# Three borders of a hybrid attention and feed-forward layer, with the work in another order: gated outputs in stages, one norm for all tokens, early fetches of sums

## The chip, the cores and the metric

One core of a Trainium2 chip runs the whole layer. The metric is the device time of one execution in microseconds; a version's time is the median of three runs. The kernel's own engines are TensorE (PE in the profile, with its weight loads as PEld), VectorE (DVE), ScalarE (ACT), GpSimd (POOL) and SyncE (SP). SP, ACT and POOL also issue the transfers between HBM and the on-chip memory.

## What is computed

The input is 256 tokens of 2048 numbers, all in fp32. `ya` is the mixed output of three groups of dilated attention with 8 heads, `o` that of a gated linear attention with 4 heads, `gr`, `m_a` and `m_b` are slices of the input's first projection.

```python
yb = (o.reshape(b, s, G_DV) * jax.nn.silu(gr)) @ w_proj_b
ya = ya.reshape(b, s, A_WIDTH) @ w_proj_a
y = jax.nn.sigmoid(m_a) * ya + jax.nn.sigmoid(m_b) * yb
x = _layernorm(ALPHA * x + y @ w_out, ln1_g, ln1_b)
ffn = (jax.nn.silu(conv(x @ w_gate)) * (x @ w_up)) @ w_down
x = _layernorm(ALPHA * x + ffn, ln2_g, ln2_b)
```

## The kernel before

**Products.** Every fp32 operand of a product is split into a rounded high part and the low rest: `split` (L138) makes the high part on ACT (L139) and the rest on DVE (L140). A product is three matmuls: high by high, high by low, low by high (L266, L267, L268 in chunks of 512 columns; L230 and L232, or L250 and L253, in tiles of 128 columns). Weights come in pieces of 512 KB, loaded by SP into a ring: `home` (L142) names the ring, either `raw` with 4 buffers or `quarter` with 12 (L851 and L1135 switch it). A piece is split into `whi` (6 buffers) and `wlo` (4 buffers). In a chunk, a piece feeds 12 matmuls: `a_chunk` (L279) runs over the pieces of 512 output columns for both halves of the tokens (t = 0, 1; 128 tokens each).

**Order.** Each engine runs its instructions in a fixed order. The order comes from a scheduler that places the instructions of the program by its own costs and dependencies; the program gives it hints. One hint is the list `side`: `pump` (L188) takes one or more entries from it after every step of a chunk (4 blocks of 128 rows), so that small work lies between the products; `drain` (L196) empties it. On-chip tiles come from rings: `blk` holds 512 numbers in each partition, `tmp` 256, `res` the large operands (8 buffers). Three pools follow each other, early, late and last, and the first user of a new pool waits for the users of the pool before it (L852, L976).

**The first border** lies behind the projections. Two chunks `m` (L845) compute the last quarter pair of `m_b`; beside them runs the rest of the last attention head. The list `side` then holds `gated_stage` (L831): fetch `gr` and `o` of one head of the gated attention (L820), multiply sigmoid(gr) by gr by o (L823), transpose the result into `OB` (L786). After that come the product with w_proj_b (chunks `pb`, L880 to L886; the operands are OB) and the product with w_proj_a (chunks `yp`, L888 on; the operands are `YA2`, which `ya_parts`, L867, fetches and splits beside the pb chunks). Their sums go into `YT`, the operands of w_out.

**The second border** is the first norm. The chunks `wo` of w_out run for n = 0, 1, 2 with both halves of the tokens; for n = 3 (L960 on) the first half of the tokens is finished first, and `normalised(0)` (L930) lies beside the products of the second half. `normalised` takes mean and scale, normalises (L935, ACT), transposes (L939, PE), applies gain and bias (L942, DVE), splits into X1 (L944 ACT, L945 DVE) and spills an fp32 copy X1F to HBM (POOL). Four matmuls on `keep` (L973) lie between.

**The third border** is the feed-forward part's start. Two groups of four pairs of tiles (`fg`, `fu`) run as plain products. Beside the second and later tiles, `sums` (L1125) prepares the operands of the seven-product scheme that the later groups use: for each of 4 quarters one entry fetches four pieces of X1F (ACT issues the transfers, L1131) and the next entry forms sums (L309 to L312, DVE) and splits them (`comb`). Later, `down_group` (L1057) accumulates the product with w_down over six parts; the sums of a part are spilled and fetched again; those of the fifth part come back into the tiles `acc` (L1160).

Of the kernel before, what the change touches and what calls it, by code (L numbers as in the profile page):

```python
# [17 lines left out]
P = 128  # L18
S = 256
D = 2048  # L20
NH = 8
# [39 lines left out]
def hybrid_layer(ctx: ExitStack, tc: tile.TileContext, wp, xt, wgl, gw, par, relb, onehot, rows, xk, out):  # L61
# [134 lines left out]
    def drain():  # L196
        while side or slow:
            pump()
# [586 lines left out]

    def transposed(name, n, halves_of_tokens, gain=None):  # L786
# [33 lines left out]
    def gated_get(h):  # L820
        got[h] = [(fetch("gr", GR[h][t]), fetch("o", O[h][t])) for t in range(2)]

    def gated_mul(h):  # L823
        for t, (x, o) in enumerate(got[h]):
            sg = blk("sg")
            nc.scalar.activation(sg, x, AF.Sigmoid)
            nc.vector.tensor_tensor(x, x, o, op=ALU.mult)
            nc.vector.tensor_tensor(sg, sg, x, op=ALU.mult)
            got[h][t] = sg

    def gated_stage(i):  # L831

        def f():
            if i < GH:
                gated_get(i)
            if 0 <= i - 1 < GH:
                gated_mul(i - 1)
            if 0 <= i - 2 < GH:
                OB.extend(transposed("ob", i - 2, got[i - 2], P_NG))
        return f  # L840


    side.extend(gated_stage(i) for i in range(GH + 2))
    for n in range(2):
        pss = a_chunk("m", xop, 16, AT["mb"] + 8 * n, 2)  # L845
        for t in range(2):
            c = blk("mc")
            nc.scalar.activation(c, pss[t], AF.Copy)
            M[1][2 + n][t] = spill("ms", c)
    drain()  # L850
    home[:] = "quarter", 12  # L851
    early.close()  # L852
    late = ExitStack()
    now[:] = late.enter_context(tc.tile_pool(name="late", bufs=1)), (17, 10, 1)
# [3 lines left out]
    def gate(br, n, t):  # L858
        g = fetch("m", M[br][n][t])
        last_gate[:] = [nc.scalar.activation(g, g, AF.Sigmoid)]  # L860
        return g


    YA2 = [res("ya") for _ in range(2)]
    yaf = {}

    def ya_parts(h):  # L867
        def f():
            if h < NH:
                yaf[h] = fetch("yaf", YA[h], tmp)  # L870
            if h:
                y = YA2[(h - 1) // 4][:, (h - 1) % 4]
                split(y[:, :S], y[:, S:], yaf[h - 1])
        return f

    side.extend(ya_parts(h) for h in range(NH + 1))
    yop = lambda kc: YA2[kc // 4][:, kc % 4]


    yb = []  # L880
    for n in range(4):
        g = [gate(1, n, t) for t in range(2)]
        pss = a_chunk("pb", by_pairs(OB), 16, AT["pb"] + 8 * n)
        for t in range(2):
            nc.vector.tensor_tensor(g[t], g[t], pss[t], op=ALU.mult)
        yb.append(g)  # L886
    drain()
    YT = []  # L888
    for n in range(4):
        g = [gate(0, n, t) for t in range(2)]  # L890
        pss = a_chunk("yp", yop, 8, AT["pa"] + 4 * n)
        for t in range(2):
            y = g[t]
            nc.vector.tensor_tensor(y, y, pss[t], op=ALU.mult)
            nc.vector.tensor_tensor(y, y, yb[n][t], op=ALU.add)
        side.append(lambda n=n, y=g: YT.extend(transposed("yt", n, y)))
# [25 lines left out]
    def residual(n, t, ps):  # L922
        r = R[t][n]
        nc.vector.scalar_tensor_tensor(r, r, ALPHA, ps, op0=ALU.mult, op1=ALU.add)
        nc.vector.bn_stats(stats[t][:, n, :], r)

    X1 = [res("x1") for _ in range(4)]
    X1F = [[None] * 4 for _ in range(2)]

    def normalised(t):  # L930

        _, rs, ms = mean_and_scale(t)
        for n in range(4):
            r = R[t][n]
            nc.scalar.activation(r, r, AF.Identity, scale=rs, bias=ms)  # L935
            pt = bank("pt")
            x1 = blk("x1f").rearrange("p (k t) -> p k t", k=4)
            for k in range(4):
                nc.tensor.transpose(pt[:, k * P : (k + 1) * P], r[:, k * P : (k + 1) * P], ident)  # L939
            for k in range(4):  # L940
                d = 4 * n + k
                nc.vector.tensor_scalar(x1[:, k], pt[:, k * P : (k + 1) * P], pc(P_L1G + d), pc(P_L1B + d), op0=ALU.mult, op1=ALU.add)  # L942
            hi, lo = X1[n][:, :, t * P : (t + 1) * P], X1[n][:, :, S + t * P : S + (t + 1) * P]
            main = nc.scalar.activation(hi, x1, AF.Copy)  # L944
            nc.vector.tensor_tensor(lo, x1, hi.bitcast(F32), op=ALU.subtract)  # L945
            X1F[t][n] = spill("x1s", x1)
            if n == 2:
                held = main
        return held

    yt = by_pairs(YT)
    for n in range(4):
        for t in range(2):
            R[t].append(blk("r"))
            nc.gpsimd.dma_start(R[t][n], xk[t * P : (t + 1) * P, n * 512 : (n + 1) * 512])
        if n < 3:
            pss = a_chunk("wo", yt, 16, AT["wo"] + 8 * n)
            for t in range(2):
                residual(n, t, pss[t])
# [361 lines left out]
```

## Time and profile before

| | |
|---|---|
| median of 3 runs | 1906.82 us (1903.97 to 1907.84) |
| the profiled execution | 1901.4 us, its span 1899.4 us |
| PE busy | 1826.8 us (96%), its clock 0.988 of full in the mean |
| DVE busy | 1449.1 us (76%) |
| ACT busy | 1089.3 us (57%) |
| DMA | 480.64 MB, 253 GB/s in the mean |

72.6 us of the span are without a matmul. In the PE's row of the 40 slices of the span, nearly all of them show 9 tenths; which stretches are not filled is read from the idle time before each group of matmuls and from windows of a few microseconds.

### The profile page before, as it was taken

Reading aid. Unit: us, or ns where it says so; the run is one execution under the profiler, and the core shown is the slowest. Engines: PE = TensorE matmul, PEld = TensorE weight load, DVE = VectorE, ACT = ScalarE, POOL = GpSimd, SP = SyncE. Lnnn points to the kernel's source line nnn. Section 1 sums busy time; section 2 is a strip of 40 time slices with the busy share of each in tenths; the row PEclk is TensorE's granted clock in tenths of the full one; section 3 lists DMA queues with packets and bytes.
Section 4 is the critical chain, followed back from the end, with each engine's and each line's share of the span. In section 5 each row is a group of like instructions: output and inputs, shape, how many; then the busy total and the mean of one; then the engine's idle time right before and its main releaser. Section 6 shows DMA issues by size and latency. Waiting matters only on the chain.

```text
span 1899.4 us, 25463 instructions
## 1 busy us (share of the span) xinstructions
PE 1826.8 (96%) x8974; PEld 1525.4 (80%) x8974; DVE 1449.1 (76%) x1731; ACT 1089.3 (57%) x1400; POOL 236.5 (12%) x349
## 2 busy tenths in 40 slices
PE   8999998999999999998999999899999999999996
PEld 6877887888888888886888878788888888888784
DVE  6968997788797978964656666786597787877977
ACT  6655765565666657654644445565565556555552
POOL 0112111111111311101300000001011110110211
PEclk9999999999999999999999999999999999999998
DMA  8898987978889897897766437569679769778683
GB/s 302 277 304 231 302 283 215 324 213 294 279 249 334 216 316 255 255 333 240 285 220 219 166 112 276 190 172 323 225 203 340 241 199 343 222 232 331 200 283 120
DMA packets 148492, 480.64 MB, mean 253 GB/s; under 512 B 17905, under 2 KB 30220, under 8 KB 148364
## 3 DMA queue, kind: packets, MB, share of 16 engines
q1 hardware_dynamic: 96764, 345.09, 50.9%
q0 software_dynamic: 33456, 115.48, 24.8%
q10 hardware_dynamic: 18144, 18.46, 3.1%
q8 instruction: 70, 1.15, 0.2%
q14 instruction: 58, 0.48, 0.1%
HBM read 383.46 MB, written 33.72 MB: 220 GB/s over the span
## 4 chain that ended last, share of the span: by engine, by line
PE 70%; DMA 9%; DVE 8%; issue 4%; ACT 2%; POOL 1%; ACTq 0%; DVEq 0%; POOLq 0%; SPq 0%
PE qk L230 7%; PE qk L232 4%; DVE wlo L140 3%; PE wd_t L267 3%; PE wd_t L268 3%; PE wd_t L266 3%; PE fu L230 3%; PE fg L230 3%; PE fguE L337 2%; DMA quarter<-in_wp 2%; PE fguA L337 2%; DMA raw<-in_wp 2%; PE fu L232 2%; PE pb_t L268 1%; PE pb_t L267 1%
## 5 line engine op out<-in xcount | busy, mean ns | idle before, releaser
L140 DVE TENSOR_TENSOR wlo<-quarter,whi 128x1024 fp32r<-128x1024 f32 x500 | 598.4, 1221 | 206.3 <-issue 54.7
L139 ACT ACTIVATE whi<-quarter 128x1024 fp32r<-128x1024 f32 x500 | 520.4, 1057 | 293.6 <-DVE quarter L350 54.4
L139 ACT ACTIVATE whi<-raw 128x1024 fp32r<-128x1024 f32 (+1 forms) x330 | 342.9, 1051 | 261.3 <-DMA raw<-in_wp 124.2
L140 DVE TENSOR_TENSOR wlo<-raw,whi 128x1024 fp32r<-128x1024 f32 (+1 forms) x330 | 395.5, 1215 | 106.7 <-ACT whi L139 53.7
L230 PE MATMUL qk<-x,whi 128*128 128x512 f32 x768 | 192.2, 399 | 0.0
L353 POOL DMA_DIRECT2D quarter<-quarter x120 | 105.3, 901 | 665.0 <-DMA quarter<-in_wp 148.5
L230 PEld LDWEIGHTS qk<-x,whi 128*128 128x128 f32 x768 | 141.8, 188 | 29.4 <-issue 1.4
L350 DVE TENSOR_TENSOR quarter<-quarter,quarter 128x1024 f32<-128x1024 f32 x120 | 143.2, 1219 | 0.3
L267 PE MATMUL wd_t<-wlo,h 128*128 128x512 f32 x352 | 137.7, 391 | 0.6 <-DVE wlo L140 0.6
L266 PE MATMUL wd_t<-whi,h 128*128 128x512 f32 x352 | 137.3, 392 | 0.3 <-ACT h L139 0.2
L268 PE MATMUL wd_t<-whi,h 128*128 128x512 f32 x352 | 136.9, 389 | 0.0
L232 PEld LDWEIGHTS qk<-x,wlo 128*128 128x128 f32 x768 | 98.8, 192 | 7.7 <-DVE wlo L140 3.9
L232 PE MATMUL qk<-x,wlo 128*128 128x256 f32 x768 | 100.5, 284 | 3.5 <-DVE wlo L140 3.5
L230 PE MATMUL fg<-x,whi 128*128 128x512 f32 x352 | 87.1, 401 | 7.7 <-DVE pa L990 7.7
L230 PE MATMUL fu<-x,whi 128*128 128x512 f32 x368 | 88.0, 391 | 0.7 <-DVE gc L1004 0.5
L230 PEld LDWEIGHTS fg<-x,whi 128*128 128x128 f32 x352 | 67.5, 194 | 22.4 <-DVE pa L990 8.3
L230 PEld LDWEIGHTS fu<-x,whi 128*128 128x128 f32 x368 | 68.2, 188 | 15.7 <-PE pt L1045 1.1
L267 PEld LDWEIGHTS wd_t<-wlo,h 128*128 128x128 f32 x352 | 66.2, 188 | 14.0 <-DVE wlo L140 1.2
L268 PEld LDWEIGHTS wd_t<-whi,h 128*128 128x128 f32 x352 | 66.1, 188 | 13.9 <-DVE h L140 0.2
L266 PEld LDWEIGHTS wd_t<-whi,h 128*128 128x128 f32 x352 | 65.9, 188 | 14.1 <-ACT h L139 0.9
L230 PE MATMUL gqk<-x,whi 128*128 128x512 f32 x256 | 66.3, 412 | 3.9 <-ACT whi L139 3.5
L230 PEld LDWEIGHTS gqk<-x,whi 128*128 128x128 f32 x256 | 50.3, 200 | 17.7 <-ACT whi L139 7.3
(361 smaller groups left out, 3194.5 us busy)
## 6 DMA issues: line engine op xcount, KB each, us to landing
raw<-in_wp SPq DMA_DIRECT2D x326, 512.0 KB, 5.4
quarter<-in_wp SPq DMA_DIRECT2D x320, 512.0 KB, 7.1
quarter<-quarter POOLq DMA_DIRECT2D x120, 512.0 KB, 9.0
af<-acc POOLq DMA_DIRECT2D x32, 256.0 KB, 6.5
acc<-af POOLq DMA_DIRECT2D x32, 256.0 KB, 5.7
sp<-c POOLq DMA_DIRECT2D x14, 256.0 KB, 8.7
bias<-bvd ACTq DMA_DIRECT2D x32, 96.0 KB, 5.3
v<-vs ACTq DMA_DIRECT2D x24, 128.0 KB, 7.3
```

Of the source, the lines that this page charges most:

```text
L139: nc.scalar.activation(hi, src, AF.Copy)
L140: nc.vector.tensor_tensor(lo, src, hi.bitcast(F32), op=ALU.subtract)
L230: nc.tensor.matmul(ps, parts(kc)[0], opnd(kc), start=(kc == 0), stop=False)
L232: nc.tensor.matmul(ps[:, S:], parts(kc)[1], opnd(kc)[:, :S], start=False, stop=(kc == nk - 1))
L266: nc.tensor.matmul(ps, xh, hi, start=first, stop=False)
L267: nc.tensor.matmul(ps, xh, lo, start=False, stop=False)
L268: nc.tensor.matmul(ps, xl, hi, start=False, stop=last)
L337: nc.tensor.matmul(ps, a(kc)[which], w[:, k * 512 : (k + 1) * 512], start=(first and w is hi and which == 0 and kc == 0), stop=(w is lo an ...
L350: tt(a, a, b, op=ALU.add)
L353: nc.gpsimd.dma_start(a, b, accum_op=ALU.add)
```

## The change

At the first border the order of the two products is turned round. `YA2` is fetched and split beside the two m chunks (three entries of `side` for each step, not two). Then the late pool opens, the first `gr`, `o` and gate tiles are fetched, and the yp chunks run first; fetching, multiplying and transposing the gated outputs is staged over the eight steps of the yp chunks, and the pb chunks come after. The gates are fetched one chunk ahead, and their sigmoid stands behind the chunk's products in the program. The ring `quarter` is named only from the pb chunks on; the yp chunks use `raw`.

At the second border the fourth wo chunk is like the other three, and the norm is made for both halves of the tokens at once: per quarter n the two halves are normalised, transposed in pairs of blocks, and gain and bias are applied to 256 columns at a time. X1F is kept in eight tiles of two blocks and 256 tokens.

At the third border each quarter's sum is fetched by two POOL transfers (not four ACT transfers), one or two entries of `side` before it is used. The first down part's fp32 copy is fetched by POOL too. In the last part but one, the sums of n = 2 and 3 stay on the chip, so that four spills and four fetches are gone.

```diff
+    side.extend(ya_parts(h) for h in range(NH))
     for n in range(2):
-        pss = a_chunk("m", xop, 16, AT["mb"] + 8 * n, 2)
+        pss = a_chunk("m", xop, 16, AT["mb"] + 8 * n, 3)
...
+    side.extend([
+        lambda: None, mul(0), both(turn(0), get(2)), mul(1),
+        both(turn(1), get(3)), mul(2), both(turn(2), mul(3)), turn(3),
+    ])
+    ya = []
+    for n in range(4):
+        g = next(ahead_of)
+        pss = a_chunk("yp", yop, 8, AT["pa"] + 4 * n)
+        gated_by(g, pss)
+        ya.append(g)
     drain()
     home[:] = "quarter", 12
...
-        if n < 3:
-            pss = a_chunk("wo", yt, 16, AT["wo"] + 8 * n)
-    pcs = [two_parts(load(AT["wo"] + 24 + k), spare=(k > 3)) for k in range(8)]
-    for t in range(2):
...
-        held = normalised(t)
+        pss = a_chunk("wo", by_pairs(YT), 16, AT["wo"] + 8 * n)
...
+    norm = [mean_and_scale(t) for t in range(2)]
+    for n in range(4):
+        for t in range(2):
+            nc.scalar.activation(r, r, AF.Identity, scale=rs, bias=ms)
+        for k in range(0, 4, 2):
...
+            X1F.append(spill("x1s", x1))
...
-                    nc.scalar.dma_start(b, X1F[t][h // 2][:, 2 * (h % 2) : 2 * (h % 2) + 2])
+                pair = fetch("x1p", X1F[h])
...
+    sums = [sums_get(0), idle, sums_get(1), sums_part(0), idle, sums_get(2), sums_part(1), idle, sums_get(3), sums_part(2), idle, sums_part(3)]
...
+                elif part == len(FSPLIT) - 2 and n > 1:
+                    F[t][n] = a
```

**PE behind the m chunks.** Before, PE's row holds the last attention head's transposes and mixes (`ppt`, `po`) behind the last m matmul, then the transposes of the gated output (`pt`) ahead of the first pb matmul:

```order
L268 MATMUL m_t_1027_7906<-whi_8064,x_86 128x512
L491 MATMUL ppt_8080<-ident,s_1016_7849 128x128
L494 MATMUL ppt_8080<-ident,s_1017_7850 128x128 x2
L506 MATMUL po_8086<-pT_8042,v_8034 128x256
L507 MATMUL po_8086<-pT_8042,v_8034 128x128
L491 MATMUL ppt_8097<-ident,s_1016_7849 128x128
L494 MATMUL ppt_8097<-ident,s_1017_7850 128x128 x2
L506 MATMUL po_8086<-pT_8084,v_8034 128x256
L507 MATMUL po_8086<-pT_8084,v_8034 128x128
L506 MATMUL po_8086<-pT_8101,v_8034 128x256
L507 MATMUL po_8086<-pT_8101,v_8034 128x128
L795 MATMUL pt_8152<-ident,sg_8127 128x128
```

In the change the last mix stands 24 matmuls ahead of the end of the m chunks, yp follows at once, and the first transposes of a gated output stand behind 75 matmuls of yp (48 of its first chunk, 27 of its second):

```order
L267 MATMUL yp_t_1089_8263<-wlo_8331,ya_7729 128x512
L268 MATMUL yp_t_1089_8263<-whi_8330,ya_7729 128x512
L817 MATMUL pt_8302<-ident,sg_8247 128x128
L817 MATMUL pt_8311<-ident,sg_8247 128x128
L266 MATMUL yp_t_1090_8264<-whi_8330,ya_7729 128x512
L817 MATMUL pt_8302<-ident,sg_8248 128x128
```

**ACT in the yp chunks.** In the change ACT's row has the sigmoids of the first gated output (`sg`) and of four gate tiles (`m`) between two high parts of weights; whi_8402 is the second piece of the third yp chunk and whi_8447 the third:

```order
L139 ACTIVATE whi_8402<-raw_8400 128x1024
L851 ACT_TABLE_LOAD
L851 ACTIVATE sg_8247<-gr_8149 128x512
L851 ACTIVATE sg_8248<-gr_8153 128x512
L884 ACTIVATE m_8165<-m_8165 128x512
L884 ACTIVATE m_8167<-m_8167 128x512
L884 ACTIVATE m_8169<-m_8169 128x512
L884 ACTIVATE m_8171<-m_8171 128x512
L139 ACTIVATE whi_8447<-raw_8445 128x1024
L824 ACTIVATE ob_8301<-pt_8302,prm 128x256
```

Before, the first sigmoids of gr stood ahead of the weights of the pb chunks, with no product beside them. What PE does meanwhile is the second yp chunk.

**The fetches of the sums.** Before, ACT's row issues the third quarter's four transfers (`x1p`) directly behind the activation of one tile:

```order
L1000 ACTIVATE gc_10580<-gc_10580 128x256
L1131 DMA x1p_10585<-x1s_9908 128x256
L1131 DMA x1p_10585<-x1s_10031 128x256
L1131 DMA x1p_10588<-x1s_9938 128x256
L1131 DMA x1p_10588<-x1s_10061 128x256
L989 ACTIVATE pa_10637<-fu_10603 128x256
```

In the change all eight stand in POOL's row directly behind the last spill of X1F (`x1s`):

```order
L112 DMA x1s_10044<-x1f_10036 128x512
L117 DMA x1p_10317<-x1s_9954 128x512
L117 DMA x1p_10319<-x1s_10006 128x512
L117 DMA x1p_10425<-x1s_9966 128x512
L117 DMA x1p_10427<-x1s_10018 128x512
L117 DMA x1p_10601<-x1s_9980 128x512
L117 DMA x1p_10603<-x1s_10032 128x512
L117 DMA x1p_10778<-x1s_9992 128x512
L117 DMA x1p_10780<-x1s_10044 128x512
L117 DMA x1f_10969<-x1s_9954 128x512
```

On DVE the first quarter's sum (L309) stands directly behind the eighth tile's sum, two tiles later than before, and the sums of the four quarters are spread over more tiles.

## Rows read from the trace of the kernel before

**Rows 1.** What PE waited for: total us, times, longest us.
```profile
PE pt L795 <- DVE sg L828: 9.1, 1, 9.1
PE fg L230 <- DVE pa L990: 7.7, 3, 4.5
PE pt L939 <- ACT r L935: 3.8, 1, 3.8
```

**Rows 2.** Windows: start:end, us, each engine's busy us, PEclk, DMA share, GB/s.
```profile
840.00:889.73 49.73, 49.73 (x235) 41.27 (x234) 25.68 (x32) 23.79 (x28) 1.62 (x3) 1.00 0.72 246
889.73:904.70 14.97, 5.08 (x27) 3.81 (x24) 5.14 (x8) 7.45 (x12) 9.60 (x18) 0.72 0.88 304
928.00:938.00 10.00, 10.00 (x46) 8.29 (x45) 7.78 (x12) 7.11 (x13) 5.74 (x12) 1.00 1.03 390
1132.48:1143.63 11.15, 6.49 (x21) 3.45 (x19) 8.44 (x18) 5.63 (x9) 1.18 (x3) 0.78 0.74 270
```

**Rows 3.** Timeline of PE, first border: start us, us, instruction [idle before <-releaser].
```profile
902.73 2.05 PE L795 MATMUL pt<-ident,sg 128*128 128x128 f32 x8 [9.14 <-DVE sg L828]
904.70 0.80 PE L266 MATMUL pb_t<-whi,ob 128*128 128x512 f32 x1
...
907.09 0.40 PE L266 MATMUL pb_t<-whi,ob 128*128 128x512 f32 x1
...
908.01 1.04 PE L795 MATMUL pt<-ident,sg 128*128 128x128 f32 x8
```

**Rows 4.** Timeline of POOL and of ACT at the first border.
```profile
893.10 0.54 POOL L117 DMA_DIRECT2D gr<-sp  x1
...
897.29 1.28 ACT L826 ACT_TABLE_LOAD   x1 [3.28 <-DMA gr<-sp]
```

**Rows 5.** DMA issues, 885 to 930 us: queue, count, KB each, median us to landing.
```profile
gr<-sp POOLq DMA_DIRECT2D x8, 256.0 KB, 4.8
...
yaf<-yas POOLq DMA_DIRECT2D x8, 128.0 KB, 6.4
...
ms<-mc POOLq DMA_DIRECT2D x2, 256.0 KB, 3.5
yas<-ya POOLq DMA_DIRECT2D x1, 128.0 KB, 3.2
```

**Rows 6.** DMA issues of the raw ring, 833 to 893 us.
```profile
raw<-in_wp SPq DMA_DIRECT2D x18, 512.0 KB, 3.7
```

**Rows 7.** The tile raw, all of its loads over the span.
```profile
DMA to landing us min/median/max: 3.1/5.4/16.4
```

**Rows 8.** Timeline of PE, second border.
```profile
1132.09 0.39 PE L268 MATMUL wo_t<-whi,yt 128*128 128x512 f32 x1
...
1143.63 0.79 PE L250 MATMUL fg<-x,whi 128*128 128x512 f32 x1 [0.21 <-DVE x L945]
```

**Rows 9.** Timeline of DVE (two rows) and ACT (one), second border.
```profile
1133.69 0.68 DVE L924 SCALAR_TENSOR_TENSOR r<-r,wo_t 128x512 f32<-128x512 f32 x1
...
1137.76 0.26 DVE L914 BATCH_NORM_AGGREGATE mv<-st 128x2 f32<-128x24 f32 x1
...
1138.80 2.93 ACT L935 ACTIVATE r<-r,ms,rs 128x512 f32<-128x512 f32 x4 [0.23 <-DVE ms L919]
```

**Rows 10.** Timeline of DVE, third border, the fourth quarter's first sum.
```profile
1226.95 0.43 DVE L309 TENSOR_TENSOR comb<-x1p,x1p 128x256 f32<-128x256 f32 x1 [5.22 <-DMA x1p<-x1s]
```

**Rows 11.** Timeline of PE, third border: four of the tiles' first halves.
```profile
1161.76 3.82 PE L230 MATMUL fu<-x,whi 128*128 128x512 f32 x16
...
1167.32 3.82 PE L230 MATMUL fg<-x,whi 128*128 128x512 f32 x16
...
1231.71 6.74 PE L230 MATMUL fg<-x,whi 128*128 128x512 f32 x16 [4.55 <-DVE pa L990]
...
1240.19 3.82 PE L230 MATMUL fu<-x,whi 128*128 128x512 f32 x16
```

**Rows 12.** Timeline of DVE at the end: the last part's first sums.
```profile
1871.30 1.28 DVE L1075 TENSOR_TENSOR acc<-acc,wd_t 128x512 f32<-128x512 f32 x2 [0.83 <-PE wd_t L268]
```

More of the change, by code (lines that the diff above doesn't have):

```diff
@@ L784, in hybrid_layer, with ya_parts, f @@
             done += 1
+    YA2 = [res("ya") for _ in range(2)]
+    def ya_parts(h):
+        def f():
+            y = YA2[h // 4][:, h % 4]
+            split(y[:, :S], y[:, S:], fetch("yaf", YA[h], tmp))
+        return f
+    side.extend(ya_parts(h) for h in range(NH))
+    yop = lambda kc: YA2[kc // 4][:, kc % 4]
+    for n in range(2):
+        pss = a_chunk("m", xop, 16, AT["mb"] + 8 * n, 3)
+        for t in range(2):
+            c = blk("mc")
+            nc.scalar.activation(c, pss[t], AF.Copy)
+            M[1][2 + n][t] = spill("ms", c)
+    drain()
+    early.close()
+    late = ExitStack()
+    now[:] = late.enter_context(tc.tile_pool(name="late", bufs=1)), (17, 10, 1)
     def transposed(name, n, halves_of_tokens, gain=None):
@@ L820, in gated_get, with f @@
     def gated_get(h):
-        got[h] = [(fetch("gr", GR[h][t]), fetch("o", O[h][t])) for t in range(2)]
+        def f():
+            got[h] = [[fetch("gr", GR[h][t]), fetch("o", O[h][t])] for t in range(2)]
+        return f
     def gated_mul(h):
[L824 to L829, printed above, removed]
@@ new lines, in gated_mul, with gated_turn, f, both @@
+        return f
+    def gated_turn(h):
+        def f():
+            OB.extend(transposed("ob", h, got[h], P_NG))
+        return f
+    def both(*fs):
+        def f():
+            for g in fs:
+                g()
+        return f
+    last_gate = []
+    def gates_ahead():
+        ahead = None
+        for br in range(2):
+            for n in range(4):
+                new = [fetch("m", M[br][n][t]) for t in range(2)]
+                if br or n:
+                    yield ahead
+                ahead = new
+        yield ahead
@@ L850, in hybrid_layer @@
+    for n in range(4):
[3 more added lines that the diff above has]
+        ya.append(g)
     drain()
     home[:] = "quarter", 12
-    early.close()
-    late = ExitStack()
-    now[:] = late.enter_context(tc.tile_pool(name="late", bufs=1)), (17, 10, 1)
-    last_gate = []
[L858 to L886, printed above, removed]
@@ L920, in mean_and_scale @@
         return mv[:, 0:1], rs, ms
[L922 to L951, printed above, removed]
     for n in range(4):
@@ L955, in hybrid_layer @@
             nc.gpsimd.dma_start(R[t][n], xk[t * P : (t + 1) * P, n * 512 : (n + 1) * 512])
-        if n < 3:
-            pss = a_chunk("wo", yt, 16, AT["wo"] + 8 * n)
-            for t in range(2):
-                residual(n, t, pss[t])
-    pcs = [two_parts(load(AT["wo"] + 24 + k), spare=(k > 3)) for k in range(8)]
-    for t in range(2):
-        ps = cbank(f"wo_t{t}")
-        for k0 in range(8):
-            hi, lo = pcs[k0]
-            for k in range(2):
-                w = slice(k * 512, (k + 1) * 512)
-                kc = 2 * k0 + k
-                a_part(ps, yt(kc), hi[:, w], lo[:, w], t, kc == 0, kc == 15)
-        residual(3, t, ps)
-        if t:
-            keep = bank("keep")
-            for _ in range(4):
-                nc.tensor.matmul(keep, ident, R[0][2], start=True, stop=True)
-        held = normalised(t)
+        pss = a_chunk("wo", by_pairs(YT), 16, AT["wo"] + 8 * n)
@@ L1052, in unit_group @@
         return seven("fgu", X1, comb1, AT["fgu", f0], keep_it), [turned(f) for f in range(f0, f0 + 4)]
-    F = []
+    F = [[None] * 4 for _ in range(2)]
     ACC = [[None] * 4 for _ in range(2)]
@@ L1143, in hybrid_layer @@
                     if not k and n == 3:
-                        side.extend(f for j in range(4) for f in sums(j))
+                        side.extend(sums)
                     if k or n > 3:
```

95 lines of the change are left out of this document (64 added, 31 removed).

## The prediction

> **What bounds the kernel now.** I read the view of PE's waits first, since PE is busy in almost every slice and its gaps are the time to be had. It names few causes [rows 1]: a transpose that waits 9.1 us for the gated output, three tiles that wait 7.7 us together for DVE, and a transpose that waits 3.8 us for the normalised tokens. They lie at the three borders that the change touches, one each. Then I read windows around each gap: between the end of the m chunks at 889.73 us and the first pb matmul at 904.70 us, PE is busy for 5.08 of 14.97 us [rows 2], while in the m chunks just before it has no gap at all. The window from the end of the wo chunks to the first tile (11.15 us) is filled for 6.49 us, and part of that is the four dummy matmuls on keep. Last I read PE's and DVE's timelines there, to see what each gap costs beyond its idle time. After the first gap the matmuls run at half pace: from 904.70 to 907.09 us six of them start in 2.39 us, and eight transposes take 2.05 us where eight take 1.04 us soon after [rows 3]. The granted clock of the gap's window is 0.72, that of the m chunks 1.00 [rows 2]: this is 1.2 instead of 2.4 GHz for some microseconds after the gap.
>
> The sum below is made against the profiled execution, 1901.4 us. The median of the runs shown is 1906.82 us, 5.4 us more; I carry the difference over to that median. A measurement of this kernel tells about 0.2%, 4 us, from no change.
>
> **First border: products turned round.** A matmul of 512 columns starts every 0.227 us at full clock (12 matmuls of a weight piece: 2.73 us; I take it from the 235 matmuls and their like that fill 49.73 us without a gap [rows 2] and from the starts in the timeline). Removed is the stretch from 889.73 to 904.70 us. Its work stays: 5.08 us busy, less 1.0 us because its eight transposes take 1.04 at full clock, so 4.1 us move into the chunks and 10.9 us go. Behind it, six matmuls take 2.39 us where 6 x 0.227 = 1.36 do [rows 3]: 1.0 us more. Together **11.9 us**, if yp really runs from the end of the m chunks without a gap.
>
> Two chains can give some of it back. Count from that end, M. First, yp needs the last head's part of YA2 at its 43rd matmul, M + 9.5 us. The last mix stands 24 matmuls ahead of the end (M - 5.5), and behind it come a copy, a spill that lands in 3.2 us, a fetch that lands in 6.4 us [rows 5], and about 2 us of copy, two issues and a split (estimated from an issue of 0.54 us [rows 4]): M + 6.1. It just fits. Second, the late pool opens only when the last users of the early one are through: the m spills (a copy behind M, then 3.5 us [rows 5]) and that last split. So the first gr fetch is issued at about M + 7 instead of 3.4 us behind M as before (893.10 us [rows 4]). Four fetches at 0.54 us an issue, 4.8 us to land [rows 4, 5]: M + 14. From the table load's start to the first transpose took 5.4 us before (897.29 to 902.73 us [rows 3, 4]), part of it waiting for the later fetches, so the gated output is there at M + 16 to M + 19; PE comes to its transposes after 75 matmuls, M + 17. A wait of 0 to 2 us there, and as much once more where ACT holds a piece of weights behind the gate tiles' sigmoids: the twelfth fetch lands at about M + 22, PE needs that piece at about M + 30. The price of both is between 0 and, if spill, fetch and gates all land like the slowest row [rows 7], some 8 us. I take 2, near the medians. Net **-9.9 us**.
>
> The yp chunks now use the ring raw with 4 buffers, where it was quarter with 12. In the m chunks the same ring feeds PE without a gap [rows 2], with loads that land in 3.7 us [rows 6]. A buffer's round is the landing plus about 2.3 us for the two halves of the split; four of them give a piece every 1.5 us there. The yp stretch, however, also carries gr, o and all gate tiles: 16 pieces of 512 KB and up to 32 fetches of 256 KB, 16.8 MB. At the 390 GB/s that a loaded stretch moved with PE full [rows 2] this is 43 us, and yp takes 16 x 2.73 = 44 us. So the stretch is full but not over-full by the trace, and I cost it at nothing. The Trainium skill (DMA: Bandwidth & Descriptors, section "Issuing engines are not separate DMA queues") speaks against that: transfers issued by different engines run on the same 16 DMA engines and interleave, so POOL's fetches are no second road. By that rule, with an even share of 195 GB/s, a load lands after 10.8 us and a piece comes every 3.3 us instead of 2.73 while the fetches last; the sum would be some 4 us worse over eight pieces, if the pieces already split (four, 11 us of matmuls) did not cover it. No row here shows this stretch with four buffers; it is the rival below.
>
> **Second border: one norm.** What moves: 16 transposes of the first half of the tokens leave the last wo chunk, about 0.1 us each there [rows 3], so that chunk ends 1.6 us sooner, and 14 of them come back into the first tiles' matmuls (+1.4). What is exposed: from the last wo matmul (1132.09 us) to the first tile (1143.63 us [rows 8]) lie residual, statistics, the small chain of 1.04 us from mean to normalised block (1137.76 to 1138.80 us [rows 9]), transposes, gain and split. Now two halves pass this: one more small chain, about 1 us, and the second half's block comes fourth on ACT (2.93 us for four [rows 9]), 2.2 us later. Against that, the residual no longer waits behind the first half's gain work on DVE: it started at 1133.69 us, 1.2 us behind the matmuls' end, and its chain had 4 us to the mean [rows 9]; I give back 2.5 us. Sum: -1.6 + 1.4 + 1 + 2.2 - 2.5 = **+0.5 us**. Bounds: -3 (DVE finds no weight to split between) and +5 (the tiles run at 1.2 GHz for longer, as 11.15 us with little work already have a clock of 0.78 [rows 2]).
>
> **Third border: sums fetched ahead.** Undisturbed, one tile takes 5.56 us (1161.76 to 1167.32 us). From 1161.76 to 1240.19 us are 12 tiles, 78.4 us instead of 66.8 [rows 11]: 11.6 us too much, of which 7.7 are idle [rows 1] and the rest the 1.2 GHz behind them (one tile's first half took 6.74 us for 3.82 [rows 11]). DVE's wait for the fetched quarters starts it, 5.22 us for the last one [rows 10]; the tile's own sum stands behind it. In the change all eight fetches are issued behind the last spill, about 25 us ahead of their first use, so the wait goes. The sums stay (eight instructions a quarter on DVE), but lie further apart. Next late is DVE itself at the last quarter, whose sums stand ahead of a weight piece of the first seven-product: about 1 us, bounds 0 and 4. Net **-10.6 us**.
>
> **The rest.** Four spills and four fetches less at the end: the last sums on DVE wait for PE, not for them [rows 12], so nothing. Sum: -9.9 + 0.5 - 10.6 = **-20 us**: 1881 us for the profiled execution, **1887 us** as a median.
>
> **The rivals.**
> - **The first border gives half back.** The chain of spill, fetch and sigmoid lands as late as its slow rows, PE stands still once for over 3 us in yp and pays 1.2 GHz again. For it: ACT, DVE and POOL are in order, and the late pool's first fetch waits for everything early. Against: 75 matmuls of cover. It costs 6 to 8 us more: 1894 us.
> - **The norm's chain grows.** All 32 transposes, 16 gain steps and 8 splits lie open; at +5 instead of +0.5, and another 1 or 2 us of slow clock: 1893 us.
> - **The ring of four starves yp; slower.** Place: the 16 pieces of yp. If a load lands like the slowest raw row, 16.4 us [rows 7], a piece comes every (16.4 + 2.3) / 4 = 4.7 us; with such gaps the clock falls and 12 matmuls take 12 x 0.4 = 4.8 us themselves. 16 x (4.8 - 2.73) = 33 us, and if the pieces ahead cover nothing, -20 + 33 = +13: 1920 us. It decides from a mean landing of 8.6 us (4 x 2.73 - 2.3); the gain is gone at about 13 us, where a piece takes 3.9 us. For it: the skill's rule above; against it: 3.7 us under 246 GB/s [rows 2, 6] and a full PE at 390 GB/s, though with twelve buffers.
> - **It doesn't do what it says.** The wait for gated outputs only moves to the front of yp (the last head's spill and fetch are late by as much), leaving the third border alone: about 1897 us.
>
> **Chances.** Forecast 0.62 (own range 1881 to 1891), half given back 0.16, norm's chain 0.10, only the third border 0.06, starving 0.06. Faster by over 0.2% are all but the last and a sliver: 0.92; within 0.2%: 0.03; slower: 0.05. The range takes the forecast with its bounds (no give-back and the short norm: 1880) and the two likeliest rivals up to 1896.
>
> **What would show it.** Right: no gap over 2 us between m and yp, the granted clock at 1.00 there; the view of DVE's waits without x1p; tiles of 5.6 us up to the first seven-product; the stretch from the last wo matmul to the first tile within 2 us of 11.5. Wrong: raw loads landing after 8 us or more with ACT waiting for them in yp; POOL's first gr fetch later than 12 us behind the m chunks; PE waiting for `sg` or for `ya`; a tile stretch that still takes over 72 us for 12 tiles.

## The result, and the profile after the change

The changed kernel takes 1890.7 us (median of 6 runs, 1884.9 to 1895.7; the kernel before beside it 1904.0): a ratio of 0.993, 95% interval 0.991 to 0.995, so 13.3 us faster. The forecast was 1887 us, 20 us faster. Direction and range hold; as a gain, the sum was too large by half. The profiled execution took 1894.0 us:

```profile
span 1892.3 us, 25421 instructions
PE 1824.9 (96%) x8974; PEld 1523.2 (80%) x8974; DVE 1446.7 (76%) x1715; ACT 1088.3 (58%) x1400; POOL 243.5 (13%) x361
```

PE's waits around the first border, from the first yp matmul to the first pb matmul (answer to [rows 1]: the wait of 9.1 us there is gone, the 7.7 us of the tiles too, but four waits have taken their place):

```profile
PE pt L817 <- DVE ob L825: 4.6, 2, 3.0
PE pt L817 <- issue: 2.3, 1, 2.3
PE yp_t L267 <- DVE wlo L140: 1.1, 1, 1.1
PE pt L817 <- DVE sg L854: 1.1, 2, 0.9
```

The first gated output is late by 2.3 us (the view names `issue`, but DVE's product `sg` for it starts at 913.7 us and PE goes on at 914.48), the second head's by 1.1 us, a piece of weights by 1.1 us; the 4.6 us lie at the end of yp. Windows of that stretch (columns as in [rows 2]): the two m chunks, yp, the place between yp and pb, the first microseconds of pb, the rest of pb:

```profile
845.50:895.00 49.50, 49.50 (x232) 41.12 (x231) 25.67 (x31) 24.99 (x32) 5.14 (x10) 1.00 0.71 238
895.00:946.70 51.70, 47.22 (x217) 38.16 (x215) 37.50 (x54) 33.31 (x53) 19.00 (x36) 1.00 0.88 301
946.70:952.80 6.10, 1.49 (x9) 1.16 (x9) 3.43 (x7) 3.96 (x8) 0.00 (x0) 0.87 0.95 347
952.80:958.10 5.30, 5.30 (x15) 4.14 (x14) 3.42 (x7) 3.15 (x7) 1.07 (x2) 0.50 0.69 258
958.10:1045.10 87.00, 87.00 (x397) 72.31 (x396) 49.05 (x50) 37.72 (x39) 3.77 (x7) 1.00 0.65 204
```

The m chunks run into yp without a gap, as forecast. yp loses 4.5 us, and between yp and pb lies a new hole of 6.1 us with 1.49 us of work. Behind it the clock is 0.50, 1.2 GHz, for 5.3 us. PE's and ACT's timelines there show who was late:

```profile
949.84 0.63 PE L817 MATMUL pt<-ident,sg 128*128 128x128 f32 x4 [2.99 <-DVE ob L825]
952.09 1.08 PE L817 MATMUL pt<-ident,sg 128*128 128x128 f32 x4 [1.62 <-DVE ob L825]
```

```profile
947.59 1.23 ACT L884 ACTIVATE m<-m 128x512 f32<-128x512 f32 x2 [2.78 <-DMA m<-sp]
948.72 0.46 ACT L824 ACTIVATE ob<-pt,prm 128x256 fp32r<-128x256 f32 x1
950.43 0.63 ACT L884 ACTIVATE m<-m 128x512 f32<-128x512 f32 x1 [1.25 <-DMA m<-ms]
950.97 0.46 ACT L824 ACTIVATE ob<-pt,prm 128x256 fp32r<-128x256 f32 x1
```

The transposes wait for a bank that `ob` has to empty; `ob` (L824) stands on ACT behind sigmoids of gates (L884), and these wait for their DMA. By ACT's order these gates belong to the second and third pb chunk, which by the length of pb (92 us for four) end some 50 and 70 us later. Their fetches had been issued late. POOL's row shows three kinds of wait: the opening of the late pool (the first line), the landing of earlier fetches (the lines at 908.23 and 910.76 us), and the buffers of the ring `blk`, which DVE's products give back (the last two lines, gates of pb):

```profile
903.44 0.54 POOL L117 DMA_DIRECT2D gr<-sp  x1 [5.33 <-PE yp_t L268]
...
907.15 0.54 POOL L117 DMA_DIRECT2D o<-os  x1
908.23 0.54 POOL L117 DMA_DIRECT2D m<-sp  x1 [0.54 <-DMA gr<-sp]
910.76 0.55 POOL L117 DMA_DIRECT2D m<-sp  x1 [2.00 <-DMA o<-os]
...
935.35 0.54 POOL L117 DMA_DIRECT2D m<-sp  x1 [6.38 <-DVE sg L854]
...
943.21 1.14 POOL L117 DMA_DIRECT2D m<-sp  x2 [5.14 <-DVE gr L852]
```

Behind eight fetches issued one after another (903.44 to 907.15 us), each of the next six, gates of yp, waited until a `gr` or an `o` tile had landed. ring22 (below) has five buffers more, and the same six waits stand in its POOL row (0.38 to 0.94 us); so they are not the ring's. What sets the number eight no run shows.

ACT stands in the same way at the start of yp, with a piece of weights behind these gates:

```profile
909.09 0.64 ACT L851 ACTIVATE sg<-gr 128x512 f32<-128x512 f32 x1
912.01 0.63 ACT L851 ACTIVATE sg<-gr 128x512 f32<-128x512 f32 x1 [2.28 <-DMA gr<-sp]
918.45 2.62 ACT L884 ACTIVATE m<-m 128x512 f32<-128x512 f32 x4 [5.81 <-DMA m<-sp]
```

The loads into the ring of four landed in 7.2 us in yp, against 3.7 us in the m chunks before [rows 6]:

```profile
raw<-in_wp SPq DMA_DIRECT2D x13, 512.0 KB, 7.2
```

At the second border the last wo matmul and the first tile stand 12.4 us apart (11.5 before [rows 8]), and the second half's small chain ends 2.0 us behind the first's:

```profile
1132.92 0.39 PE L268 MATMUL wo_t<-whi,yt 128*128 128x512 f32 x1
...
1145.31 0.80 PE L250 MATMUL fg<-x,whi 128*128 128x512 f32 x1
```

```profile
1137.50 0.14 DVE L936 SCALAR_TENSOR_TENSOR ms<-mv,rs 128x1 f32<-128x1 f32 x1
...
1139.51 0.16 DVE L936 SCALAR_TENSOR_TENSOR ms<-mv,rs 128x1 f32<-128x1 f32 x1 [1.62 <-ACT rs L934]
```

At the third border a tile takes 5.57 us, and 12 tiles 67.3 us (78.4 before [rows 11]). The last quarter's sum starts without a wait (5.22 us before [rows 10]):

```profile
1166.03 3.82 PE L230 MATMUL fu<-x,whi 128*128 128x512 f32 x16
...
1171.60 3.82 PE L230 MATMUL fg<-x,whi 128*128 128x512 f32 x16
...
1233.30 3.82 PE L230 MATMUL fu<-x,whi 128*128 128x512 f32 x16
...
1246.38 0.73 PE L337 MATMUL fguA<-wlo,x 128*128 128x512 f32 x2 [1.43 <-DVE wlo L140]
```

```profile
1229.42 0.42 DVE L309 TENSOR_TENSOR comb<-x1p,x1p 128x256 f32<-128x256 f32 x1
```

**How the runs are compared.** One kernel's runs scatter by up to 16 us, more than most terms here. So each run is also cut into stretches at starts on PE's timeline: the first matmul of the last two m chunks, the first wo matmul, the first fu tile whose 16 matmuls stand together (L230), the first seven-product (fguA), the end. The columns are the lengths in us; the names are those of the experiments below.

| profile | start to m | m to wo | wo to fu | fu to seven | seven to end |
|---|---|---|---|---|---|
| before | 842.7 | 199.5 | 119.6 | 84.0 | 653.7 |
| changed | 845.5 | 199.6 | 120.9 | 72.8 | 653.4 |
| changed, again | 843.2 | 196.0 | 120.3 | 72.5 | 653.2 |
| border1_alone | 845.9 | 194.7 | 120.9 | 82.2 | 656.9 |
| border2_alone | 850.0 | 200.6 | 120.0 | 85.9 | 656.3 |
| border3_alone | 842.7 | 199.6 | 121.0 | 72.5 | 655.9 |
| sums_not_kept | 844.1 | 196.9 | 120.1 | 72.4 | 655.3 |
| gates_behind | 847.3 | 193.2 | 119.8 | 72.4 | 653.3 |
| ring22 | 840.9 | 194.4 | 120.3 | 73.9 | 653.2 |
| turned_later | 846.7 | 196.2 | 120.3 | 73.6 | 653.4 |
| yp_from_quarter | 845.6 | 195.5 | 119.9 | 73.5 | 654.8 |
| sigmoids_in_need | 844.5 | 191.2 | 121.2 | 73.1 | 653.5 |
| in_need_quarter | 847.0 | 188.4 | 121.2 | 74.9 | 652.7 |
| in_need_old_norm | 843.9 | 187.4 | 120.0 | 73.0 | 654.8 |

PE's instructions ahead of m are the same in number (4105 or 4106 matmuls recorded), and no edit lies there; yet that stretch scatters by 9 us. Its mean is 845 us with the old and with the new first border, so the scatter is none of the change's doing.

### The profile page after: what moved, and what is told of

It reads as the page before. It is cut to its first block, busy times and chain, and to the rows that moved or that the text cites. A ratio compares the mean times of both kernels' runs of the same rounds, so it can differ in the third digit from the quotient of the medians.

```text
span 1892.3 us, 25421 instructions
## 1 busy us (share of the span) xinstructions
PE 1824.9 (96%) x8974; PEld 1523.2 (80%) x8974; DVE 1446.7 (76%) x1715; ACT 1088.3 (58%) x1400; POOL 243.5 (13%) x361
## 4 chain that ended last, share of the span: by engine, by line
PE 69%; DMA 10%; DVE 9%; issue 4%; ACT 2%; POOL 1%; ACTq 0%; DVEq 0%; SPq 0%; POOLq 0%
PE qk L230 7%; DVE wlo L140 4%; PE wd_t L267 4%; PE wd_t L266 4%; PE wd_t L268 4%; PE qk L232 4%; PE fu L230 3%; PE fguE L337 3%; DMA quarter<-in_wp 3%; PE fg L230 3%; PE fguA L337 2%; DMA raw<-in_wp 2%; PE fguD L337 2%; PE mE L337 2%; PE pb_t L267 2%
## 5 line engine op out<-in xcount | busy, mean ns | idle before, releaser
L140 DVE TENSOR_TENSOR wlo<-quarter,whi 128x1024 fp32r<-128x1024 f32 x484 | 579.4, 1221 | 207.4 <-issue 61.1
L139 ACT ACTIVATE whi<-quarter 128x1024 fp32r<-128x1024 f32 x484 | 505.4, 1058 | 300.4 <-DVE quarter L350 58.5
L139 ACT ACTIVATE whi<-raw 128x1024 fp32r<-128x1024 f32 (+1 forms) x346 | 359.6, 1053 | 257.7 <-DMA raw<-in_wp 119.8
L140 DVE TENSOR_TENSOR wlo<-raw,whi 128x1024 fp32r<-128x1024 f32 (+1 forms) x346 | 414.4, 1215 | 112.8 <-ACT whi L139 49.6
L230 PE MATMUL qk<-x,whi 128*128 128x512 f32 x768 | 192.2, 399 | 0.0
L230 PEld LDWEIGHTS qk<-x,whi 128*128 128x128 f32 x768 | 141.9, 188 | 29.4 <-issue 1.4
L230 PE MATMUL fu<-x,whi 128*128 128x512 f32 x368 | 88.0, 391 | 0.5 <-DVE gc L1004 0.4
L230 PE MATMUL fg<-x,whi 128*128 128x512 f32 x352 | 84.0, 390 | 0.0
L230 PEld LDWEIGHTS fu<-x,whi 128*128 128x128 f32 x368 | 68.2, 188 | 15.3 <-PE pt L1045 1.2
L230 PEld LDWEIGHTS fg<-x,whi 128*128 128x128 f32 x352 | 65.5, 188 | 13.3
L230 PE MATMUL gqk<-x,whi 128*128 128x512 f32 x256 | 65.7, 409 | 4.4 <-ACT whi L139 3.6
L230 PEld LDWEIGHTS gqk<-x,whi 128*128 128x128 f32 x256 | 50.2, 200 | 17.8 <-ACT whi L139 7.4
```

The source lines that it names most:

```text
L139: nc.scalar.activation(hi, src, AF.Copy)
L140: nc.vector.tensor_tensor(lo, src, hi.bitcast(F32), op=ALU.subtract)
L230: nc.tensor.matmul(ps, parts(kc)[0], opnd(kc), start=(kc == 0), stop=False)
```

## The experiments

**One border at a time.** The first three kernels are the kernel before with one part of the change; the fourth is the changed kernel with one line more.

border1_alone: the hunks of the diff from `YA2` to the pb chunks, nothing else.

> The kernel before with only the first border's new order (yp ahead of pb, gated outputs in stages, gates fetched one chunk ahead). Theory A (what the first border gained at its own place was given back inside the next 60 us: PE waits about 4.5 us in yp, about 4.6 us between yp and pb, and pays the 1.2 GHz clock behind that): 1900 to 1905 us against 1904 before, PE waits of 3 to 6 us in all for the gated output of the last head, and from the start of the m chunks to the first wo matmul 199 us as before. Theory B (the border did gain the forecast 10 us and the trace of the whole change hides it under scatter elsewhere): 1894 us, and that stretch takes 190 us.

1905.8 us (1900.3 to 1911.3; ratio 1.0006, 0.9992 to 1.002): no gain. By the total this is theory A, a little above its range. The stretch from m to wo is 194.7 us, between the theories: 4.8 us were gained in this profile. PE waits in yp as in the changed kernel (3.7 us in three waits), but between yp and pb lie 1.6 us and not 6, with 0.3 us of waiting for `ob`. How much is given back differs by execution: the changed kernel itself, profiled again below, waits 2.3 us there, not 4.6, and the clock behind stays at 1.00.

border2_alone: `norm` for both halves and the new X1F; the sums still fetched late by ACT (two halves of a tile each).

> The kernel before with only the one norm for all tokens (and the new shape of X1F, its fetches still late and by ACT). Theory A: the norm costs about what its stretch shows in the profile of the changed kernel, +1 to +2 us: 1905 to 1906 us. Theory B (it costs nothing or gains, the +1 being the changed layout's or scatter): 1901 to 1904 us. The rival of a grown chain (+5): 1909 us, with the stretch from the last wo matmul to the first tile above 14 us.

1906.8 us (ratio 1.0012, 0.9994 to 1.003), too wide to tell 0 from 5 us. The profiled run took 1914 us, 7 us of it ahead of m. Its wo to fu is 120.0 us, 0.4 more than before, and from the last wo matmul to the first tile are 12.4 us, not over 14 as the rival has it; so the rival of +5 falls.

border3_alone:

```diff
-                    nc.scalar.dma_start(b, X1F[t][h // 2][:, 2 * (h % 2) : 2 * (h % 2) + 2])
+                    nc.gpsimd.dma_start(q, X1F[t][h // 2][:, 2 * (h % 2) : 2 * (h % 2) + 2])
...
-                        side.extend(f for j in range(4) for f in sums(j))
+                        side.extend(sums)
```

> The kernel before with only the fetches of the sums moved: issued by POOL (four transfers a quarter as before), in the staged order of the change; norm, spills and the end as before. Theory A (the third border gives its 11 us to the end of the program): 1893 us, 12 tiles in 67 us, no wait for x1p on DVE. Theory B (the fetches were only part of it: half comes back where the seven-products start): 12 tiles in 67 us and yet 1897 to 1899 us, with a PE wait of over 3 us for weights or sums at the first seven-product.

1896.5 us (ratio 0.996, 0.995 to 0.997): 8.4 us, between the theories. The stretch fu to seven is 72.5 us instead of 84.0, 11.5 us less, and PE's wait at the first seven-product is 1.0 us, not over 3: theory A's mechanism, and B's falls. What total and stretch differ by stands in the stretch to the end (655.9 us), which scatters from 653.7 to 656.9 us in the kernels with that part of the program as before.

gates_behind:

```diff
...
-        for x in g:
-            last_gate[:] = [nc.scalar.activation(x, x, AF.Sigmoid)]
+        with tc.issue_after(last_high[0].ins):
+            for x in g:
+                last_gate[:] = [nc.scalar.activation(x, x, AF.Sigmoid)]
```

`last_high` is the last high part of weights made before, which is that of the chunk's own last piece.

> The changed kernel with one thing more: the sigmoids of a chunk's gates may not stand on ACT ahead of the last high part of that chunk's own weights. Theory A (ACT, in order, stood with the sigmoids of gates needed 30 to 70 us later, whose fetches were late, while the last gated output waited behind them): the PE waits between yp and pb fall from 4.6 to under 1 us, the clock stays at 1.00 there, and the time falls by 6 to 8 us to 1883 to 1885 us. Theory B (the stretch is held up by the transfers themselves, the DMA engines being full): the waits only move to another instruction, 1889 to 1892 us, as the change.

1889.2 us (1885.7 to 1891.1; ratio 0.992, 0.990 to 0.994): 1.5 us better than the change, which the intervals can't tell from it; by the total this is theory B. In the place it aimed at, the waits for `ob` are 1.1 us, and the clock behind is 1.00:

```profile
PE pt L819 <- issue: 2.7, 1, 2.7
PE pt L819 <- DVE ob L827: 1.1, 2, 0.9
PE yp_t L269 <- DVE wlo L142: 0.5, 1, 0.5
```

That alone does not show the cause, since without this line the five profiles of the order have 0.3 to 4.6 us there (mean 2.7). With ACT's timeline of the first profile, and with ring22 below, which has this line too and no wait for `ob` there, it speaks for ACT's order as the cause of the hole between yp and pb. The size was wrong: the first gated output is as late as before.

**Later transposes, more buffers.** turned_later and ring22 start from gates_behind.

```diff
-... tc.tile_pool(name="late", bufs=1)), (17, 10, 1)
+... tc.tile_pool(name="late", bufs=1)), (22, 10, 1)
...
-        lambda: None, mul(0), both(turn(0), get(2)), mul(1),
+        lambda: None, lambda: None, mul(0), both(turn(0), get(2)), mul(1),
...
-    drain()
     home[:] = "quarter", 12
```

> The kernel of the run before (gates' sigmoids behind their chunk's own weights) with a ring blk of 22 buffers in the late pool, not 17, and with the gated outputs one step later: their first transposes stand behind 96 matmuls of yp, not 75, and those of the last head behind the first 24 matmuls of pb. Theory A (what is left of the loss at the first border, 4.3 us of idle PE and 1.5 us of slow clock between the start of m and the first wo matmul, is the first gated output being fetched too late for 75 matmuls): PE idles under 1.5 us there, the stretch takes 188 to 189 us instead of 193.2, and the time falls by 4 to 5 us to 1884 or 1885 us. Theory B (the transfers of that stretch, 15.7 MB in 52 us, hold it up whoever waits): the stretch stays at 192 us or more, 1888 to 1890 us.

1889.7 us (1888.4 to 1891.9; ratio 0.992, 0.991 to 0.994), m to wo 196.2 us: the numbers of theory B. But the place is another than B has it. The gated output was not ready 96 matmuls behind m either, and PE waited 6.08 us at one place. ACT's timeline says why:

```profile
908.87 1.06 ACT L141 ACTIVATE whi<-raw 128x1024 fp32r<-128x1024 f32 x1 [0.81 <-DVE wlo L142]
919.42 1.28 ACT L887 ACT_TABLE_LOAD   x1 [9.49 <-DMA m<-sp]
920.72 1.15 ACT L887 ACTIVATE m<-m 128x512 f32<-128x512 f32 x2
921.77 0.61 ACT L853 ACTIVATE sg<-gr 128x512 f32<-128x512 f32 x1
```

With the later entry the scheduler put the first gates' sigmoids ahead of `sg`; ACT stood 9.49 us for a gate, though by POOL's row the first `gr` had landed by 910.5 us. The move had turned the order it was meant to help.

ring22 is the first line of that diff alone.

> The kernel with the gates' sigmoids held back, and with the ring blk of 22 buffers as its only other difference; the gated outputs are not moved. Theory A (POOL's waits for buffers of that ring, 6.4 and 5.1 us, hurt only because ACT waited for the gates behind them; with the sigmoids held back they hurt no more): no change against 1889 us, the wait of 2.7 us at the first gated output stays. Theory B (the late buffers themselves are the bound): the waits in yp go, 1885 to 1887 us.

1886.1 us (1882.3 to 1893.6; ratio 0.991, 0.989 to 0.993). m to wo is 194.4 us, no better than gates_behind's 193.2, and three waits in yp still come to 3.8 us; the lower total stands ahead of m (840.9 us, the lowest of all). I read this as theory A for the stretch; the total can't tell.

**The ring of four, and the end.** Both start from the changed kernel.

yp_from_quarter: `home[:] = "quarter", 12` stands ahead of the yp chunks.

> The changed kernel with the ring of twelve buffers (quarter) named ahead of the yp chunks, not behind them, so that the weights of yp are loaded up to twelve pieces ahead. Theory A (four buffers were enough: raw landed in 7.2 us there, less than the 8.6 us at which the ring would set the pace): no change within 2 us of 1890.7 us, or 1 to 3 us slower since the gated outputs and gates then share the DMA engines with more loads. Theory B (the ring of four held yp up): yp shorter by 2 us or more, 1886 to 1888 us.

1891.2 us (1889.1 to 1894.5; ratio 0.993, 0.992 to 0.995): no change. m to wo is 195.5 us, within the 194.7 to 199.6 us of the changed order. The ring of four did not hold yp up: theory A.

sums_not_kept:

```diff
-                elif part == len(FSPLIT) - 2 and n > 1:
-                    F[t][n] = a
...
-            for n in range(2):
+            for n in range(4):
                 for t in range(2):
```

> The changed kernel with the last sums of the part before the last spilled and fetched again, as before the change (8 spills and 8 fetches instead of 4 and 4). The prediction's term for this was nothing: then 1890.7 us within 2 us, and from the first seven-product to the end 653 us as in both profiles. Rival: the transfers cost 2 to 3 us at the end, 1893 us, and that stretch takes 656 us.

1897.1 us (1890.5 to 1900.2; ratio 0.996, 0.994 to 0.997). The rival holds: seven to end is 655.3 us. In all five profiles in which these sums go out and come back this stretch is 653.7 to 656.9 us (mean 655.6), in the nine others 652.7 to 654.8 (mean 653.6). The place is the transposes of the last groups: from the first seven-product to the end PE's waits for `gc` there come to 2.1 to 3.2 us in the five and to 1.1 to 1.7 us in the nine. The longest, first in this kernel, then in the changed one:

```profile
1851.18 0.33 PE L1045 MATMUL pt<-ident,c 128*128 128x128 f32 x1 [2.21 <-DVE gc L1004]
```

```profile
1857.40 0.33 PE L1045 MATMUL pt<-ident,c 128*128 128x128 f32 x1 [0.47 <-DVE gc L1004]
```

`gc` comes by way of ACT (L997, L1000), and ACT issues one of the fetches between the two, having stood for a weight load ahead of both:

```profile
1846.74 1.06 ACT L139 ACTIVATE whi<-raw 128x1024 fp32r<-128x1024 f32 x1 [1.31 <-DMA raw<-in_wp]
...
1849.82 0.33 ACTq L1170 DMA_DIRECT2D acc<-acc  x1
1850.25 0.72 ACT L1000 ACTIVATE gc<-gc 128x256 f32<-128x256 f32 x2 [1.54 <-DVE gc L999]
1851.65 0.33 ACTq L1170 DMA_DIRECT2D acc<-acc  x1
1852.02 0.72 ACT L139 ACTIVATE h<-gc 128x256 fp32r<-128x256 f32 x2 [1.04 <-DMA acc<-af]
```

The wait of 1.04 us for a spill ends after that transpose has started; it can only bear on PE's next wait, 0.65 us for ACT's `h`. How the 2 us divide between the late load, the issue and the spill is not shown. The median is 6 us above the change's where the stretch says 2; the rest stays open.

**The order of need.** change_again is the changed kernel itself.

> The changed kernel itself once more, for a second profile of its first border and a closer time beside the next kernel. Theory A (its loss there depends on how late the gate tiles land in an execution, since ACT stands behind their sigmoids; three profiles of this order gave 194.7, 196.9 and 199.6 us from the start of m to the first wo matmul): 194 to 200 us again, 1889 to 1892 us in all. Rival (the 199.6 us of its first profile were an outlier and the border gains its forecast 10 us as a rule): 190 us there and 1884 to 1887 us in all.

1891.2 us (1886.9 to 1895.1; ratio 0.993, 0.992 to 0.995), m to wo 196.0 us: theory A.

sigmoids_in_need starts from ring22:

```diff
+                else:
+                    gated_get(1)()
...
+        with tc.issue_after(high.ins):
...
-        lambda: None, mul(0), both(turn(0), get(2)), mul(1),
-        both(turn(1), get(3)), mul(2), both(turn(2), mul(3)), turn(3),
+        lambda: None, mul(0), get(2), both(turn(0), mul(1)),
+        get(3), both(turn(1), mul(2)), mul(3), turn(2), turn(3),
...
+        if n:
+            gated_by(*late_gate, sg_of[0] if n == 1 else weights[-3])
+        late_gate = g, pss
...
```

> The changed kernel with the first border's small work in the order of need: ring blk of 22 buffers; POOL fetches the first chunk's gates ahead of the second gated head; the first gates' sigmoids stand behind those of the first gated output, later ones behind weights of the next chunk; the first transposes stand behind 96 matmuls of yp and the last head's behind 24 of pb. Transfers are as many as in the change. Theory A (ACT's order, not the transfers, was the loss; the run with later transposes failed since a gate's sigmoid stood ahead of the gated output's and held ACT for 9.5 us): PE idles under 2 us between m and wo at clock 1.00, that stretch takes 188 to 190 us, and the time is 1882 to 1885 us. Theory B (15.7 MB in 52 us are the bound, someone always waits 3 to 6 us): 193 us or more, 1887 to 1890 us.

1884.6 us (1884.5 to 1885.2; ratio 0.990, 0.988 to 0.991), 6.6 us under the changed kernel on the same chip, whose interval it does not touch. The windows of its m, yp, border and pb:

```profile
844.50:894.60 50.10, 49.66 (x232) 41.06 (x231) 25.70 (x31) 25.39 (x33) 4.99 (x10) 1.00 0.69 234
894.60:944.20 49.60, 46.26 (x210) 37.69 (x209) 36.90 (x53) 32.17 (x50) 20.65 (x39) 1.00 0.95 338
944.20:945.00 0.80, 0.80 (x9) 0.77 (x8) 0.80 (x2) 0.52 (x1) 0.00 (x0) 1.00 1.04 420
945.00:1035.70 90.70, 90.70 (x419) 75.51 (x418) 55.06 (x62) 44.77 (x55) 3.22 (x6) 1.00 0.64 218
```

As many transfers, and no wait for a gated output, and no slow clock: the order of the small work was the larger part of the loss, and not the amount that is moved, theory A. The edit also moves the first gates' fetches ahead of the second head's on POOL and the transposes to a later step, so ACT's part is not parted from these. The idle 3.8 us are more than its 2 and m to wo is 191.2, not 188 to 190: the waits left are mostly for weights, behind ACT's 2.7 and 1.3 us for loads under a DMA share of 0.95. That much speaks for B.

in_need_quarter: as yp_from_quarter, on top of this.

> The kernel of the run before (small work in the order of need, 1884.6 us) with the ring of twelve buffers named ahead of the yp chunks. What is left there are three PE waits of 0.9 to 1.3 us for weights, ACT having stood 2.7 and 1.3 us for loads into the ring of four. Theory A (those waits come from the four buffers, now that ACT no longer stands elsewhere): they go, m to wo takes 188 to 189 us instead of 191.2, and the time is 1882 us. Theory B (the transfers share the DMA engines, so that loads made earlier push the gated outputs and gates later): 191 us or more, 1884 to 1887 us.

1884.5 us (1880.5 to 1886.0; ratio 0.989, 0.987 to 0.991): the same. Its m to wo is 188.4 us as A has it, but the next kernel reaches 187.4 us with the ring of four, so this is not settled.

in_need_old_norm: the norm and X1F of the kernel before, on sigmoids_in_need.

> The kernel with the small work in the order of need (1884.6 us), with the norm of the kernel before: first half of the tokens ahead of the second half's last products, X1F in its old shape (so each quarter's sum comes by four transfers, still early and by POOL). Theory A (the one norm costs or gains under 1 us; over the profiles so far the stretch from the first wo matmul to the first fu tile took 120.5 us with two norms and 120.2 with one): 1884 to 1886 us. Theory B (one norm costs 2 to 3 us, as the run with the norm alone had it, 1906.8 against 1904.9): 1882 us.

1882.2 us (1880.8 to 1882.7; ratio 0.988, 0.986 to 0.990), the best of all, 21 us under the kernel before. It looks like theory B, but wo to fu differs by only 1.2 us (120.0 to 121.2), the end takes 1.3 us longer, and the rest of the profiles' difference lies between m and wo, where the two kernels run the same instructions in one order. Whether the one norm costs 0 or 2 us stays open. Its windows are the measure of the first border:

```profile
843.90:893.40 49.50, 49.50 (x232) 41.15 (x231) 25.73 (x32) 25.41 (x34) 5.14 (x10) 1.00 0.69 234
893.40:939.80 46.40, 45.68 (x209) 37.66 (x209) 35.90 (x52) 32.13 (x49) 20.53 (x39) 1.00 0.96 358
939.80:1031.30 91.50, 91.50 (x425) 76.26 (x424) 56.58 (x63) 45.31 (x55) 3.22 (x6) 1.00 0.65 221
```

All the work from m to wo takes 186.7 us at clock 1.00 (the sum of the busy times of the three windows), and 187.4 us are reached.

## Why the forecast was right, and where it was not

- **The first border's gain: right.** Taking 11.9 us from the 199.5 us of before leaves 187.6; the last kernel, which has the small work in another order, takes 187.4, with 0.7 us of gaps and the clock at 1.00 in all three windows. The changed kernel itself does not reach it.
- **The give-back: the step that failed.** "I take 2, near the medians", with bounds 0 and 8. The four profiles of this order (changed, again, border1_alone, sums_not_kept) take 194.7 to 199.6 us: 7 to 12 us are given back, and the net is 3.1 us in the mean (199.9 to 196.8), not 9.9. In the first profile, beside the 186.7 us of work, there are 9.1 us idle (199.6 less 190.5 busy) and 3.8 us of longer busy time (190.5 less 186.7), most of it the 5.3 us at half the clock. The prediction looked at the first gated output and one piece of weights. It did not follow ACT's order to the end of yp, where the last head's `ob` stands behind gates that are needed much later, nor POOL's waits, for landings and for buffers. The dates it did work out were close: the first gr fetch stood at M + 8.4 us for "about M + 7", the wait for the first gated output was 2.3 us for "0 to 2". One of its signs of being wrong did come, PE waiting for `sg`.
- **The ring of four at nothing: right for the changed kernel.** 7.2 us is under the 8.6 us that the prediction named as decisive. Twelve buffers alone changed nothing. Whether they help once the order is mended stays open (in_need_quarter). The Trainium skill (DMA: Bandwidth & Descriptors, section "Issuing engines are not separate DMA queues") says that transfers issued by different engines interleave on the same 16. The trace agrees in kind, 7.2 us a load with POOL's fetches beside them and 3.7 us in the m chunks; the 10.8 us that the prediction made of it, by an even share, did not come.
- **The second border at +0.5 us: right, term by term.** wo to fu has a mean of 120.4 us both with the old norm (4 profiles) and with the new (10). Cut further, at the last wo matmul and at the first tile, the profiles agree closely. The wo chunks take 89.95 to 89.98 us with the old norm and 87.80 to 87.85 with the new: -2.2 for "-1.6". From the last wo matmul to the first tile are 11.54 to 11.57 us and 12.24 to 12.39 us: +0.8 for the +0.7 of "1 + 2.2 - 2.5". From there to the fu tile are 18.9 and 20.2 us in the mean: +1.4 for "+1.4". Inside the second term one guess was off: the second small chain ends 2.0 us behind the first, not 1.
- **The third border at -10.6 us: right.** 84.0 us in the mean of three profiles, 73.1 us in eleven: -10.9. The wait for x1p is gone from DVE, the give-back at the first seven-product is 1.4 us for "about 1".
- **The rest at nothing: wrong by about 2 us.** "The last sums on DVE wait for PE, not for them" looked at the sums alone. The loss lies earlier, at the transposes of the last groups, whose inputs pass ACT, and ACT issues these fetches among its activations. By the means of the stretches keeping them gains 2.0 us; which of the waits there makes it stays open.

The stretches give -3.1, 0, -10.9 and -2.0, together -16 us; the two measurements of the changed kernel give -13.3 and -12.5, with intervals down to -18 and -16. The three borders alone sum to -5.5 us by their medians (+0.9, +2.0, -8.4), and -2 to -6 us for the sums kept on the chip come to that; so the medians explain 7 to 12 us of the 13, within what they scatter. Of the rivals "half given back" is the one that happened, by its mechanism (a late sigmoid on an in-order engine) and by its price: "6 to 8 us more", and 6.8 are measured (9.9 less 3.1). The first profile gave nearly all back, with the larger wait at the end of yp, where the rival did not look. The rival's 1894 us were 12.8 us under the prediction's base of 1906.8, as the measured gains are 13.3 and 12.5. That 1890.7 us lies nearer to the forecast's 1887 is luck: the kernel before measured 2.9 us lower beside it, and keeping the sums brought 2 us that were put at nothing.

## What to carry to other kernels

Where work is moved under other work, read the in-order engine that carries both to the end of the stretch: an early fetch whose consumer stands early in ACT's row is not a free prefetch, since whatever stands behind waits for its landing. Place a consumer by the time of its need, not by the time its data might be there. And where runs scatter by more than the term in question, cut profiles into stretches that start and end at the same instructions.

## What was not expected of the hardware

- The same instructions from the start to m took between 840.9 and 850.0 us in 14 profiles; no run shows why.
- After a hole of 6.1 us in which PE was busy for 1.49 us, the granted clock was 0.50 for 5.3 us. In turned_later one wait of 6.08 us had matmuls 0.43 us apart behind it; gaps of 1.3 us and less in sigmoids_in_need left the clock at 1.00.
- Stretches with a DMA share of 0.95 and 0.96 (338 and 358 GB/s) fed PE from four buffers of weights with gaps of 3.3 us in 49.6 and of 0.7 us in 46.4.
